# The attention bias of a diffusion trunk: mask laid down by ScalarE, table added by accumulating transfers from GpSimd's queue

## The chip, the core and the metric

One core of one Trainium2 chip. The metric is the device time of one execution of the whole program in microseconds (us), the median of several runs. TensorE (PE) does the matrix products, VectorE (DVE), ScalarE (ACT) and GpSimd (POOL) the elementwise work, SyncE (SP) issues nearly all transfers. Each engine takes its instructions in a fixed order and stops at the first one whose inputs are not there.

## The reference, cut to what matters

Two layers of a trunk over 256 latent tokens (a grid of 4 rows and 64 columns) and 256 context tokens, 1024 wide. A layer is a half-step SwiGLU, a mixer, and another SwiGLU; each is normed and modulated by vectors that come from a product of the conditioning with `ada_w`. One part of the mixer is neighbourhood attention with six heads, and its scores get a bias from a small table, with a mask on columns that are too far:

```python
col_ok = (col[None, :] >= c0[:, None]) & (col[None, :] < c0[:, None] + NA_COLS)
d_row = row_idx - r[:, None]
d_col = jnp.clip(col[None, :] - col[:, None], 1 - NA_COLS, NA_COLS - 1)
bias = rpb[:, d_row[:, None, :, None] + NA_ROWS - 1, d_col[None, :, None, :] + NA_COLS - 1].astype(jnp.float32)
bias = jnp.where(col_ok[None, None, :, None, :], bias, MASK_VALUE).reshape(h, rows, GRID_W, n_keys)
s_lat = jnp.einsum('bhrqd,bhrkd->bhrqk', qg, kg).astype(jnp.float32) * scale + bias
```

All arithmetic is float32. The mask is finite (-1e30), so mask plus table value is the mask again.

## The kernel before, in words

**Weights.** Each product is made of three matmuls of split operands: a weight tile `raw` comes in by SP (line 96, three buffers), ScalarE rounds it to its high part `whi` (line 109), VectorE subtracts to get the low part `wlo` (line 110), and TensorE runs lines 224, 225 and 226. Units are converted a few ahead of their use.

**The start.** SP issues, in this order: the identity (a first slice of the constants `cc`), the tokens, eight tiles `adaraw` of `ada_w`, two `raw` tiles, eight more `adaraw`, then the rest of `cc` (line 1139, 1056 KB, which holds the column mask), the sinks, a third `raw` tile, and the table copied 64 times into DRAM scratch `scr` (line 1035, once for each layer). Meanwhile ScalarE squares the tokens, and the reciprocal norms are spread over the partitions: TensorE makes them a row (line 1264), ScalarE copies that row to `rbc` (line 1266, once for the latents and once for the context). Then for each of four blocks of modulation, TensorE multiplies (`adaps`, line 314), ScalarE evicts (`adaev`, line 317), TensorE turns the result (`adap`, line 320), VectorE adds (`mod`, line 298). With `rbc` and `mod` VectorE makes `xn` (line 1281) and ScalarE `h` (line 1283), and the first products of the first SwiGLU start. The blocks come in two pairs; half of the first products lie between the pairs.

**Later modulation** runs beside the products: VectorE multiplies and sums tiles `adaraw` into `adaacc` (lines 347, 349), in a side stream that `tick` advances by a credit for each unit of products.

**The bias.** `load_bias` stands in that side stream, once for each layer, behind the first jobs. `bias` is one tile of 12 pieces (head and half of the queries) of 128 x 256, used for both layers. 24 transfers from SP (line 1041) place the table, each 64 partitions by 4 rows of 64 elements from `scr`, shifted by one element from partition to partition. Then one addition on GpSimd (line 1044) adds the column mask to all of it. The attention reads it on VectorE (line 893); it runs in the mixer, 537 us after the start in the first layer.

**What sets the order.** A scheduler orders each engine's instructions by the order of the program and by what its own model takes to be ready; it moves the pieces of `load_bias` far ahead of the place where they are written. On GpSimd, the mixer's linear attention has its products with `tot` (line 778) and the zeroing of `atbd` (lines 819, 820), which ScalarE then fills (line 821); later come the preparation of `hp` and `ssq` (lines 1215, 1233, 1234).

Of the kernel before, what the change touches and what calls it, by code (L numbers as in the profile page):

```python
# [10 lines left out]
AF = mybir.ActivationFunctionType  # L11
OP = mybir.AluOpType
# [55 lines left out]
class Stream:  # L68
    """Weights in the order of their use: loaded ahead, split into float32r high and low parts ahead."""

# [43 lines left out]
    def pump(self, n=1):  # L114
        """Split up to n more units, no further ahead than the limit."""
        while n > 0 and self.done_conv < min(self.pos + self.au, len(self.units)):
            with Prio(self.K.tc, self.late):
                self.convert()
            n -= 1
# [9 lines left out]
def merge(*streams):  # L129
    """Interleave generators that yield their cost: each (generator, expected total)."""  # L130
    live = [[g, max(tot, 1e-6), 0.0] for g, tot in streams]
    while live:
        s = min(live, key=lambda e: e[2] / e[1])
        try:
            s[2] += next(s[0])
        except StopIteration:
            live.remove(s)


def weave(*streams):  # L140
    """Like merge, of generators that yield None while they wait for what another one traces."""
    live = [[g, max(tot, 1e-6), 0.0] for g, tot in streams]
    while live:
        for s in sorted(live, key=lambda e: e[2] / e[1]):
            try:
                c = next(s[0])
            except StopIteration:
                live.remove(s)
                break
            if c is not None:  # L150
                s[2] += c
                break
        else:
            raise AssertionError("nothing can go on")
# [12 lines left out]
class Prio:  # L167
    """Instructions traced inside count as d places later (or earlier) in the order of the program."""

# [26 lines left out]
class Kern:  # L196
# [30 lines left out]

# [1 line left out]
    def plan(self):  # L229
# [51 lines left out]

# [1 line left out]
    def ada_load(self, l, blk, q):  # L283
        """Two of the eight row chunks of a block of 512 columns."""
        src = self.ins["ada_w"]
        r = self.slot([128, 2, 512], F32, "adaraw")
        off = src[l].offset + q * 256 * 9216 + blk * 512
        self.nc.sync.dma_start(r, bass.AP(tensor=src.tensor, offset=off,
                                          ap=[[9216, 128], [128 * 9216, 2], [1, 512]]))
        return r  # L290

    def ada_put(self, l, m, bs, src):
        """mod = sums + ada_b for halves bs of m; src is [128, 4, len(bs), 2]."""
        nb = len(bs)
        col = l * 72 + m * 8 + 4 * bs[0]
        b = self.adab[:, col:col + 4 * nb].rearrange("p (b c) -> p c b", b=nb)
        dst = self.mod[l][:, m, 4 * bs[0]:4 * bs[0] + 4 * nb, :].rearrange("p (b c) t -> p c b t", b=nb)
        self.nc.vector.tensor_tensor(out=dst, in0=src, in1=b[:, :, :, None].to_broadcast([128, 4, nb, 2]), op=OP.add)
        ds = slice(4 * bs[0], 4 * bs[0] + 4 * nb)
        if m in (1, 4, 7):  # L300
            c0 = l * 24 + (m // 3) * 8
            g = self.normg[:, c0 + ds.start:c0 + ds.stop]
            self.nc.vector.scalar_tensor_tensor(self.modA[l][:, m // 3, ds, :], self.mod[l][:, m, ds, :], 1.0,
                                                g[:, :, None].to_broadcast([128, 4 * nb, 2]), op0=OP.add, op1=OP.mult)
        if m in (2, 8):
            self.nc.vector.tensor_scalar(self.mod[l][:, m, ds, :], self.mod[l][:, m, ds, :], 0.5, None, op0=OP.mult)

    def ada_direct(self, l, blk, raws):
        """All products on the tensor engine: four column groups take the row chunks in turn."""
        nc = self.nc  # L310
# [12 lines left out]
    def ada_gen(self, l, ms):  # L323
        """Products and sums over the row chunks on the vector engine, sums over partitions on the tensor engine."""
        nc = self.nc
# [63 lines left out]

# [1 line left out]
    def rstd(self, ps, n, scale):  # L391
        """1/sqrt(ps * scale + eps) for n columns of PSUM."""
        nc = self.nc
# [24 lines left out]
    def first(self, norm, us, segs, take, more=None):  # L418
        """Products of the first units after a norm. Those of the latents are of x * g * (1 + scale) and of the shift
        beside it, and the rest of the norm is applied to them; those of the context are of the normed chunks."""  # L420
        if norm.boot is not None:
# [51 lines left out]

# [1 line left out]
    def ffn(self, l, j, norm, nxt):  # L475
# [81 lines left out]
    def tail(self, units, prod, l, m, nxt):  # L557
        """The last chunks of a sublayer, one token segment after the other, with the first's norm under the second."""
        self.preload(AF.Sqrt, self.eps[:, 0:1])
# [12 lines left out]
    def preload(self, func, src):  # L572
        """Have the table of a function loaded ahead of its use, after src is there."""
        t = self.small("preload")
        self.nc.scalar.activation(t[:, 0:1], src, func)

# [1 line left out]
    def proj(self, h, n):  # L578
# [83 lines left out]
    def stack_q(self, src, n, scale):  # L662
        """Per head of a pair: its high part on its own 64 partitions, its low part on the other 64."""
        nc = self.nc
# [8 lines left out]
    def stack_k(self, src, copies):  # L673
        """Per head of a pair: its high part on both halves of the partitions; its low part on its own or both."""
        nc = self.nc
# [186 lines left out]
    def attention(self, l, R, kind):  # L862
        """Software-pipelined over (pair of heads, tile of queries)."""
        nc = self.nc
# [164 lines left out]
    def load_bias(self, l):  # L1029
        """bias[q, k] = rpb[row(k) - row(q) + 7, col(k) - col(q) + 15] + column mask, by copies one element apart."""  # L1030
        nc = self.nc
        src = self.ins["na_rpb"]
        n = 6 * 15 * 31
        scr = self.dram.tile([64, n], F32, tag="scr", name="scr")
        nc.sync.dma_start(scr, bass.AP(tensor=src.tensor, offset=src[l].offset, ap=[[0, 64], [1, n]]))
        for qt in range(2):
            for r in range(2):
                off = scr.offset + (7 - (2 * qt + r)) * 31 + 15
                dst = self.bias[r * 64:r * 64 + 64, qt:12:2, :].rearrange("p h (a b) -> p h a b", a=4)
                for h in range(6):  # L1040
                    nc.sync.dma_start(dst[:, h], bass.AP(tensor=scr.tensor, offset=off + h * 465,
                                                         ap=[[n - 1, 64], [31, 4], [1, 64]]))
                    yield 0.25
        nc.gpsimd.tensor_tensor(out=self.bias[:, 0:12, :], in0=self.bias[:, 0:12, :], op=OP.add,
                                in1=self.colmask[:, None, :].to_broadcast([128, 12, 256]))

# [1 line left out]
    def build(self):  # L1048
# [140 lines left out]
class Norm:  # L1189
    """RMSNorm with modulation: h = x * rstd * g * (1 + scale) + shift, in float32r high and low parts."""  # L1190

# [27 lines left out]
    def pre(self, d):  # L1219
        """x * g * (1 + scale) of a chunk of the latents and, after it, the shift, in high and low parts."""  # L1220
        K = self.K
        nc = K.nc
# [20 lines left out]
    def upto(self, s, n):  # L1243
        """Trace the steps of the norm of a segment up to number n: 1 rstd, 2 its row, 3 modulation."""
        while self.stage[s] < n:
# [11 lines left out]
    def spread(self, s):  # L1257
        """rstd, from a column per tile of tokens to a row on all partitions."""
        K = self.K
# [30 lines left out]
class Final(Norm):  # L1290
    """The last RMSNorm: the chunks are scaled by g and turned token-major as they come."""

# [76 lines left out]
```

## Time and profile before

| what | value |
|---|---|
| runs | 1915.71, 1918.98, 1918.99 us; median 1918.98 us |
| profiled execution, first to last instruction | 1913.9 us |
| TensorE busy | 1868.6 us, 98% of the span |
| VectorE busy | 1258.1 us, 66% |
| ScalarE busy | 722.9 us, 38% |
| GpSimd busy | 140.4 us, 7% |
| mean granted TensorE clock | 0.993 |

For the profiled execution the profile gives the span alone, no time of its own beside it; the three runs lie 1.8 to 5.1 us above that span. The busy shares are means over 1.9 ms; what a change is worth is read where an engine stands still. "Idle before" names in brackets how long an engine stood before an instruction and what ended that.

### The profile page before, as it was taken

Reading aid. Unit: us, or ns where it says so; the run is one execution under the profiler, and the core shown is the slowest. Engines: PE = TensorE matmul, PEld = TensorE weight load, DVE = VectorE, ACT = ScalarE, POOL = GpSimd, SP = SyncE. Lnnn points to the kernel's source line nnn. Section 1 sums busy time; section 2 is a strip of 40 time slices with the busy share of each in tenths; the row PEclk is TensorE's granted clock in tenths of the full one; section 3 lists DMA queues with packets and bytes.
Section 4 is the critical chain, followed back from the end, with each engine's and each line's share of the span. In section 5 each row is a group of like instructions: output and inputs, shape, how many; then the busy total and the mean of one; then the engine's idle time right before and its main releaser. Section 6 shows DMA issues by size and latency. Waiting matters only on the chain.

```text
span 1913.9 us, 27639 instructions
## 1 busy us (share of the span) xinstructions
PE 1868.6 (98%) x11023; PEld 1529.9 (80%) x11023; DVE 1258.1 (66%) x2325; ACT 722.9 (38%) x1202; POOL 140.4 (7%) x207
## 2 busy tenths in 40 slices
PE   7989999999999899999999999999999999999998
PEld 4777777889777578787777897777888977789998
DVE  4796758665865778867567675565334767687554
ACT  3332322245345357323222262222123535566443
POOL 0100000030400102000000020000001140020000
PEclk9999999999999999999999999999999999999999
DMA  9765546432311122645446327565222411146651
GB/s 342 201 217 164 164 146 205 147 110 67 89 29 36 33 70 67 220 155 175 146 149 201 121 80 229 156 203 169 88 94 82 124 54 48 31 139 203 214 172 56
DMA packets 233642, 258.24 MB, mean 135 GB/s; under 512 B 18886, under 2 KB 195370, under 8 KB 233258
## 3 DMA queue, kind: packets, MB, share of 16 engines
q1 hardware_dynamic: 233514, 256.48, 42.1%
q8 instruction: 87, 1.43, 0.3%
q14 instruction: 41, 0.34, 0.1%
HBM read 255.41 MB, written 2.48 MB: 135 GB/s over the span
## 4 chain that ended last, share of the span: by engine, by line
PE 91%; DVE 4%; ACT 2%; DMA 1%; issue 1%; SPq 1%; POOL 1%; DVEq 0%; ACTq 0%; POOLq 0%
PE mm L224 27%; PE mm L225 27%; PE mm L226 26%; PE ot L936 2%; PE pt L917 2%; PE s L882 1%; DMA adaraw<-in_ada_w_dram 1%; PE hgo L836 1%; DVE adaacc L349 1%; PE s L881 1%; PE adaps L359 1%; POOL k L778 1%; PE lv L751 0%; DVE tot L785 0%; ACT whi L109 0%
## 5 line engine op out<-in xcount | busy, mean ns | idle before, releaser
L224 PE MATMUL mm<-h,whi 128*128 128x512 f32 (+1 forms) x1632 | 594.8, 365 | 7.0 <-DVE silu L523 4.8
L225 PE MATMUL mm<-h,wlo 128*128 128x512 f32 (+1 forms) x1632 | 589.6, 362 | 0.0
L226 PE MATMUL mm<-h,whi 128*128 128x512 f32 (+1 forms) x1632 | 589.5, 361 | 0.0
L110 DVE TENSOR_TENSOR wlo<-raw,whi 128x1024 fp32r<-128x1024 f32 (+2 forms) x344 | 400.2, 1183 | 91.7 <-ACT whi L109 76.9
L109 ACT ACTIVATE whi<-raw 128x1024 fp32r<-128x1024 f32 (+2 forms) x344 | 338.7, 1012 | 296.4 <-PE mm L225 130.1
L224 PEld LDWEIGHTS mm<-h,whi 128*128 128x128 f32 x1632 | 307.7, 189 | 69.7 <-issue 15.0
L225 PEld LDWEIGHTS mm<-h,wlo 128*128 128x128 f32 x1632 | 307.9, 189 | 50.9 <-issue 2.5
L226 PEld LDWEIGHTS mm<-h,whi 128*128 128x128 f32 x1632 | 307.6, 189 | 50.5 <-issue 0.7
L349 DVE SCALAR_TENSOR_TENSOR adaacc<-adaraw,s,adaacc 128x512 f32<-128x512 f32 x392 | 281.8, 765 | 37.2 <-DMA adaraw<-in_ada_w_dram 35.9
L224 PE MATMUL mm<-g,whi 128*128 128x512 f32 (+1 forms) x740 | 265.3, 359 | 0.0
L226 PE MATMUL mm<-g,whi 128*128 128x512 f32 (+1 forms) x740 | 264.0, 357 | 0.0
L225 PE MATMUL mm<-g,wlo 128*128 128x512 f32 (+1 forms) x740 | 263.8, 357 | 0.0
L219 ACT ACTIVATE g<-silu 128x512 fp32r<-128x512 f32 (+1 forms) x92 | 51.4, 562 | 320.5 <-DVE silu L523 287.9
L523 DVE TENSOR_TENSOR silu<-mm,silu 128x512 f32<-128x512 f32 (+1 forms) x80 | 50.0, 630 | 167.2 <-PE mm L226 142.4
L224 PEld LDWEIGHTS mm<-g,whi 128*128 128x128 f32 x740 | 139.3, 188 | 24.8 <-ACT whi L109 2.5
L415 DVE SCALAR_TENSOR_TENSOR xT<-mm,mod,xT 128x256 f32<-128x256 f32 x216 | 96.7, 478 | 94.6 <-PE mm L226 94.0
L225 PEld LDWEIGHTS mm<-g,wlo 128*128 128x128 f32 x740 | 139.3, 188 | 21.6
L226 PEld LDWEIGHTS mm<-g,whi 128*128 128x128 f32 x740 | 139.3, 188 | 21.6
L1233 POOL CAST hp<-mod 128x2 fp32r<-128x2 f32 x40 | 22.3, 588 | 1073.1 <-PE mm L225 338.9
L522 ACT ACTIVATE silu<-mm 128x512 f32<-128x512 f32 (+1 forms) x80 | 42.7, 548 | 130.5 <-PE mm L226 130.5
L220 DVE TENSOR_TENSOR g<-silu,g 128x512 fp32r<-128x512 f32 (+1 forms) x92 | 54.9, 604 | 31.9 <-ACT g L219 31.6
L1215 POOL TENSOR_TENSOR ssq<-ssq,sq 128x256 f32<-128x256 f32 x50 | 44.4, 902 | 309.5 <-ACT sq L1212 309.3
(213 smaller groups left out, 2016.1 us busy)
## 6 DMA issues: line engine op xcount, KB each, us to landing
raw<-in_ffn_w_dram SPq DMA_DIRECT2D x120, 1024.0 KB, 5.5
adaraw<-in_ada_w_dram SPq DMA_DIRECT2D x144, 512.0 KB, 5.2
raw<-in_ffn_w_dram SPq DMA_DIRECT2D x16, 768.0 KB, 5.2
raw<-in_w_in_dram SPq DMA_DIRECT2D x12, 1024.0 KB, 5.2
raw<-in_w_in_dram SPq DMA_DIRECT2D x16, 512.0 KB, 5.1
raw<-in_w_out_dram SPq DMA_DIRECT2D x8, 640.0 KB, 3.9
bias<-scr SPq DMA_DIRECT2D x48, 64.0 KB, 2.4
raw<-in_w_in_dram SPq DMA_DIRECT2D x4, 768.0 KB, 4.7
```

What stands on the lines that cost most here:

```text
L109: K.nc.scalar.activation(hi, v, AF.Copy)
L110: K.nc.vector.tensor_tensor(out=lo, in0=v, in1=hi.bitcast(F32), op=OP.subtract)
L219: self.nc.scalar.activation(hi, src, AF.Copy)
L220: self.nc.vector.tensor_tensor(out=lo, in0=src, in1=hi.bitcast(F32), op=OP.subtract)
L224: mmul(ps, whi, ahi, start=start, stop=False)
L225: mmul(ps, wlo, ahi, start=False, stop=False)
L226: mmul(ps, whi, alo, start=False, stop=stop)
L349: nc.vector.scalar_tensor_tensor(acc[:, t], w, sc, acc[:, t], op0=OP.mult, op1=OP.add)
L415: self.nc.vector.scalar_tensor_tensor(self.x[:, d, sl], ps[:, sl], self.mod[l][:, m, d, s:s + 1], self.x[:, d, sl], op0=OP.mult, op1=OP.add)
L522: nc.scalar.activation(a[:, 0:n], ps[i][:, 0:n], AF.Silu)
L523: nc.vector.tensor_tensor(out=a[:, 0:n], in0=ps[2 + i][:, 0:n], in1=a[:, 0:n], op=OP.mult)
L1215: eng.tensor_tensor(out=self.ssq[s], in0=self.ssq[s], in1=t, op=OP.add)
```

## The change

`load_bias` no longer adds on GpSimd. Four ScalarE activations first copy the column mask into the bias, three pieces of 256 columns each; the 24 placing transfers move from SP's queue to GpSimd's and add what they bring to what is there. The four new steps also take 2.0 of credit in the side stream. (The change takes comments and docstrings out as well; behind `load_bias`, line numbers are 2 higher.)

```diff
     def load_bias(self, l):
...
         nc.sync.dma_start(scr, bass.AP(tensor=src.tensor, offset=src[l].offset, ap=[[0, 64], [1, n]]))
+        for b in range(0, 12, 3):
+            nc.scalar.activation(self.bias[:, b:b + 3, :], self.colmask[:, None, :].to_broadcast([128, 3, 256]), AF.Copy)
+            yield 0.5
         for qt in range(2):
             for r in range(2):
                 off = scr.offset + (7 - (2 * qt + r)) * 31 + 15
                 dst = self.bias[r * 64:r * 64 + 64, qt:12:2, :].rearrange("p h (a b) -> p h a b", a=4)
                 for h in range(6):
-                    nc.sync.dma_start(dst[:, h], bass.AP(tensor=scr.tensor, offset=off + h * 465,
-                                                         ap=[[n - 1, 64], [31, 4], [1, 64]]))
+                    nc.gpsimd.dma_start(dst[:, h], bass.AP(tensor=scr.tensor, offset=off + h * 465,
+                                                           ap=[[n - 1, 64], [31, 4], [1, 64]]), accum_op=OP.add)
                     yield 0.25
-        nc.gpsimd.tensor_tensor(out=self.bias[:, 0:12, :], in0=self.bias[:, 0:12, :], op=OP.add,
-                                in1=self.colmask[:, None, :].to_broadcast([128, 12, 256]))
```

ScalarE's order at the start, before (`rs` is the reciprocal norm, `preload` loads a function table, `rbc`, `adaev` and `h` as above):

```order
L396 ACTIVATE rs<-ss,eps 128x4
L575 ACTIVATE preload<-eps 128x1
L1266 ACTIVATE rbc<-rbc 128x256 x2
L317 ACTIVATE adaev<-adaps 128x512 x2
L1283 ACTIVATE h<-xn,mod_141 128x256 x4
L109 ACTIVATE whi<-raw 128x1024 x4
```

and with the change, the same stretch:

```order
L396 ACTIVATE rs<-ss,eps 128x4
L575 ACTIVATE preload<-eps 128x1
L1038 ACTIVATE bias<-cc 128x768 x2
L1268 ACTIVATE rbc<-rbc 128x256
L1038 ACTIVATE bias<-cc 128x768
L1268 ACTIVATE rbc<-rbc 128x256
L1038 ACTIVATE bias<-cc 128x768
L317 ACTIVATE adaev<-adaps 128x512 x2
L1285 ACTIVATE h<-xn,mod_141 128x256 x4
L109 ACTIVATE whi<-raw 128x1024 x4
```

Two pieces of the mask stand ahead of the first `rbc`, two more ahead of the first `adaev`. SP's order from the second eight `adaraw` on, before:

```order
L288 DMA adaraw<-in_ada_w_dram 128x2x512 x8
L1139 DMA cc<-in_consts_dram 128x2112
L1142 DMA sink<-in_sw_sink_dram 128x12
L96 DMA raw<-in_ffn_w_dram 128x8x256
L1035 DMA scr<-in_na_rpb_dram 64x2790 x2
L1041 DMA bias<-scr 64x4x64 x5
L96 DMA raw<-in_ffn_w_dram 128x8x256 x2
L1041 DMA bias<-scr 64x4x64 x17
L96 DMA raw<-in_ffn_w_dram 128x8x256
L288 DMA adaraw<-in_ada_w_dram 128x2x512 x2
```

and with the change:

```order
L288 DMA adaraw<-in_ada_w_dram 128x2x512 x8
L1141 DMA cc<-in_consts_dram 128x2112
L1144 DMA sink<-in_sw_sink_dram 128x12
L96 DMA raw<-in_ffn_w_dram 128x8x256
L1036 DMA scr<-in_na_rpb_dram 64x2790 x2
L96 DMA raw<-in_ffn_w_dram 128x8x256 x3
L288 DMA adaraw<-in_ada_w_dram 128x2x512 x2
```

The mask's transfer keeps its place; the placing transfers are gone from this queue. GpSimd's order in the first layer's mixer, before (`k` and `tot` belong to the linear attention):

```order
L778 TENSOR_TENSOR k_3145<-k_3145,tot 128x8x32 x2
L819 MEMSET atbd 64x8x64
L820 MEMSET atbd 64x8x64
L819 MEMSET atbd 64x8x64
L820 MEMSET atbd 64x8x64
L1044 TENSOR_TENSOR bias<-bias,cc 128x3072
L1233 CAST hp<-mod_141 128x2 x2
```

and with the change:

```order
L778 TENSOR_TENSOR k_3146<-k_3146,tot 128x8x32 x2
L1045 DMA bias<-scr 64x4x64 x6
L819 MEMSET atbd 64x8x64
L820 MEMSET atbd 64x8x64
L819 MEMSET atbd 64x8x64
L820 MEMSET atbd 64x8x64
L1045 DMA bias<-scr 64x4x64 x18
L1235 CAST hp<-mod_141 128x2 x2
```

Six of the second layer's transfers now stand ahead of the zeroing of `atbd`; the second layer's four mask pieces lie on ScalarE among this mixer's softmax, the first behind its second exponential.

## Rows read from the trace of the kernel before

**Rows 1.** The page: span and busy time of TensorE.
```profile
span 1913.9 us, 27639 instructions
...
PE 1868.6 (98%) x11023; PEld 1529.9 (80%) x11023; DVE 1258.1 (66%) x2325; ACT 722.9 (38%) x1202; POOL 140.4 (7%) x207
```
**Rows 2.** Waits of TensorE, 60 to 300 us: waited for, total us, times, longest.
```profile
PE mm L224 <- DVE silu L523: 4.8, 1, 4.8
```
**Rows 3.** Waits of TensorE, 600 to 700 us.
```profile
PE pt L917 <- DVE sm L908: 5.0, 1, 5.0
```
**Rows 4.** Timeline of ScalarE, 0 to 60 us: start, length, what, idle before.
```profile
17.44 0.38 ACT L1266 ACTIVATE rbc<-rbc 128x256 f32<-128x256 f32 x1 [4.71 <-PE rbc L1264]
...
21.42 0.60 ACT L317 ACTIVATE adaev<-adaps 128x512 f32<-128x512 f32 x1 [3.02 <-PE adaps L314]
...
26.98 1.71 ACT L1283 ACTIVATE h<-xn,mod 128x256 fp32r<-128x256 f32 x4 [1.34 <-DVE mod L298]
```
**Rows 5.** Timeline of SP's queue, 0 to 100 us.
```profile
28.21 0.53 SPq L1139 DMA_DIRECT2D cc<-in_consts_dram  x1
...
50.94 14.92 SPq L1041 DMA_DIRECT2D bias<-scr  x17
```
**Rows 6.** Line 1139, the transfer that holds the mask: issue to landing.
```profile
DMA to landing us min/median/max: 13.4/13.4/13.4
```
**Rows 7.** ScalarE's groups by shape: the nearest copy of 768 columns.
```profile
L109 ACT ACTIVATE whi<-raw 128x768 fp32r<-128x768 f32 x40 | 31.9, 834 | 13.3 <-PE mm L225 13.3
```
**Rows 8.** Timeline of TensorE, 0 to 60 us.
```profile
17.91 3.43 PE L314 MATMUL adaps<-adaraw,s 128*32 128x512 f32 x16
...
25.69 1.05 PE L320 MATMUL adap<-cc,adaev 128*128 128x2 f32 x8 [0.72 <-ACT adaev L317]
28.33 3.77 PE L314 MATMUL adaps<-adaraw,s 128*32 128x512 f32 x12 [1.59 <-DMA adaraw<-in_ada_w_dram]
...
33.24 0.73 PE L224 MATMUL mm<-h,whi 128*128 128x512 f32 x2
...
38.93 0.95 PE L320 MATMUL adap<-cc,adaev 128*128 128x2 f32 x8
```
**Rows 9.** Timeline of VectorE, 0 to 60 us: the first low parts.
```profile
30.03 4.63 DVE L110 TENSOR_TENSOR wlo<-raw,whi 128x1024 fp32r<-128x1024 f32 x4
```
**Rows 10.** Stretches: us, busy (x) of PE, PEld, DVE, ACT, POOL, granted clock, DMA.
```profile
52.00:62.00 10.00, 10.00 (x37) 8.06 (x38) 8.64 (x15) 5.77 (x9) 0.00 (x0) 0.84 1.01 261
...
104.00:108.00 4.00, 4.00 (x14) 3.11 (x14) 4.00 (x7) 4.00 (x5) 0.00 (x0) 0.71 0.76 273
650.00:656.00 6.00, 5.53 (x23) 3.59 (x24) 3.48 (x13) 1.29 (x5) 0.18 (x1) 0.51 0.00 0
```
**Rows 11.** All that touches the bias: count, ns min/median/max, first and last start.
```profile
L1041 SPq DMA_DIRECT2D bias<-scr x48: 573/614/1756, 46.3 to 640.4; - x48
L893 DVE CUSTOM_DVE_ANT_1 sb<-s,bias x22: 672/692/693, 536.9 to 1639.5; 128x512 f32<-128x512 f32 x22
...
L1044 POOL TENSOR_TENSOR bias<-bias,cc x2: 6933/7154/7374, 81.8 to 643.2; 128x3072 f32<-128x3072 f32 x2
```
**Rows 12.** Timeline of VectorE, 58 to 125 us.
```profile
73.27 0.88 DVE L347 TENSOR_SCALAR adaacc<-adaraw,s 128x512 f32<-128x512 f32 x2 [7.32 <-DMA adaraw<-in_ada_w_dram]
74.07 4.06 DVE L349 SCALAR_TENSOR_TENSOR adaacc<-adaraw,s,adaacc 128x512 f32<-128x512 f32 x6
...
81.05 9.95 DVE L349 SCALAR_TENSOR_TENSOR adaacc<-adaraw,s,adaacc 128x512 f32<-128x512 f32 x5
```
**Rows 13.** Timeline of VectorE, 630 to 660 us.
```profile
643.68 6.65 DVE L909 TENSOR_SCALAR P<-P,sm 128x256 f32<-128x256 f32 x1
```
**Rows 14.** Timeline of GpSimd, 530 to 760 us.
```profile
554.46 0.52 POOL L819 MEMSET atbd<- 64x512 f32 x1 [46.47 <-PE kTps L795]
```
**Rows 15.** Timeline of ScalarE, 536 to 580 us.
```profile
541.34 0.71 ACT L904 ACTIVATE P<-sb,sm 128x512 f32<-128x512 f32 x1
...
557.28 0.63 ACT L821 ACTIVATE atbd<-at 64x512 f32<-64x512 f32 x1
```

## The prediction

> **What bounds the kernel now.** The page comes first: TensorE is busy for 98% of the span [rows 1]. So a stretch in which TensorE stands still is lost for good, and work on another engine costs nothing until TensorE waits for it. TensorE's own waits therefore come second. After the start only two are of any length: 4.8 us for VectorE's `silu` [rows 2] and 5.0 us for a `sm` of the softmax [rows 3]. Both are traces of GpSimd's additions to the bias: these last 6.9 and 7.4 us, from 81.8 us and from 643.2 us on [rows 11], and beside them five `adaacc` steps take 9.95 us, where six took 4.06 us shortly before [rows 12], and one small scaling takes 6.65 us [rows 13]. VectorE is held by the addition, and TensorE then waits for VectorE. The third look is at the start (ScalarE's and TensorE's timelines): there a chain rules that goes norm row, `rbc`, `adaps`, `adaev`, `mod`, `h`, first products, and every link stands on the order of one engine.
>
> **Part 1: the mask pieces on ScalarE at the start.** In ScalarE's order the first two pieces stand ahead of the first `rbc`. They read the part of `cc` that SP requests at 28.21 us [rows 5] and that takes 13.4 us to land [rows 6]: the mask is there at 41.6 us. Nothing ahead of that transfer in SP's order changes, so I keep this moment. In the kernel before, `rbc` ran at 17.44 us [rows 4]; ScalarE will now stand still in front of it. A piece is 768 columns; the nearest row, a copy of 768 columns, takes 0.83 us [rows 7], and I take 0.8. So `rbc` comes at 41.6 + 2 x 0.8 = 43.2 us, 25.8 us late.
>
> What follows? The first `adaps` starts at 17.91 us, just behind the first `rbc` (17.44 + 0.38), and ends at 21.34, when `adaev` starts [rows 4, 8]; I take it that `adaps` waits for `rbc`. The other two pieces (1.6 us) then lie beside `adaps` and cost nothing. Up to `h` all is 25.8 us late: 26.98 + 25.8 = 52.8 us [rows 4]. From there some of it comes back. Before, TensorE waited 1.59 us for `adaraw` and spent 28.33 to 33.24 us on `adaps` between arrivals, so the first product began 6.3 us after `h` [rows 4, 8]; with the change these tiles have long landed. Now the low parts of the weights limit: four of them, done by VectorE at 30.03 + 4.63 = 34.7 us [rows 9], and now at 60.5 us. Between 33.24 us and the next `adap` at 38.93 us lie 24 matmuls, 0.237 us each [rows 8]; in TensorE's order, which is the same in both kernels here, seven of them stand behind the fourth low part. So that `adap` comes at 60.5 + 7 x 0.237 = 62.2 us, 23.3 us late. Behind it nothing gives any back: both kernels have the same order and all transfers of the start have landed.
>
> TensorE also comes out of a long idle time. After a shorter one, before 52 us, the granted clock over the next 10 us was 0.84 [rows 10], so part of it ran at 1.2 instead of 2.4 GHz, worth 10 x 0.16 = 1.6 us. I add that. **Loss at the start: 23.3 + 1.6 = 24.9 us.** Lower end 21.8 us (23.3 less 1.5, if `adaps` doesn't wait for `rbc`); upper end 25.8 + 1.6 = 27.4 us (nothing comes back).
>
> **Part 2: GpSimd's additions go.** First layer: VectorE gets back what it lost at 81 us, 9.95 us less five steps of 4.06 / 6 us, that is 6.6 us [rows 12], more than the 4.8 us that TensorE waited. SP's queue helps: before, 17 placing transfers held it from 50.94 us for 14.92 us [rows 5], and VectorE waited 7.32 us for the `adaraw` behind them [rows 12]. So I count the whole wait, 4.8 us, and the slow clock behind it, 4 us at 0.71, 1.2 us [rows 2, 10]: 6.0 us. Second addition: 5.0 us of waiting [rows 3] and 5.5 busy us at a clock of 0.51, 2.7 us [rows 10]: 7.7 us. **Gain: 6.0 + 7.7 = 13.7 us**, with a lower end of 0, if something else is late at the same places.
>
> **Part 3: the four mask pieces in the mixer.** 4 x 0.8 us on ScalarE, which is idle more than it works there; each waits for readers of the bias that the next exponential needs too. I count one piece, 0.8 us, in the softmax chain, 0 to 3.2 us as bounds.
>
> **Part 4: 48 accumulating transfers from GpSimd.** The trace has none. The nearest row is the same transfer issued by SP: 0.61 us, at most 1.76 us [rows 11]. In the first layer 24 of them start when scratch and mask are there, and the attention reads the bias at 536.9 us [rows 11]: even at ten times SP's time they are hidden. In the mixer six go ahead of the zeroing of `atbd`. The first piece lies behind the second exponential, at about 541.3 + 0.8 = 542.1 us; the zeroing ran at 554.46 us, and ScalarE's filling, which waits for it, at 557.28 us [rows 14, 15]. So there is room for (557.3 - 0.5 - 542.1) / 6 = 2.4 us each. I take SP's longest, 1.76 us, and cost this at nothing; beyond 2.4 us it becomes a rival below. The other 18 have only `hp` behind them, much later. The 2.0 of credit move a few `adaacc` steps by a place: nothing, give or take 1 us.
>
> The Trainium skill (SBUF — State Buffer, section Who interferes with whom) says that GpSimd's writing of transfer descriptors needs a port pair that VectorE takes whole in its two-port modes, so that such a transfer looks stalled. No run here shows it for transfers. By that rule the six would take longer than by SP's row, and the sum would be the second rival's.
>
> **Sum.** 24.9 - 13.7 + 0.8 = +12.0 us. The profiled span of 1913.9 us [rows 1] becomes 1925.9 us. The runs lie 1.8 to 5.1 us above that span; I add the sum to their median: 1918.98 + 12.0 = **1931.0 us**. Ends: 1918.98 + 21.8 - 13.7 = 1927.1 us and 1918.98 + 27.4 + 3.2 = 1949.6 us.
>
> **The rivals.** *Faster: ScalarE isn't held at the start.* Then only parts 2 and 3 stand, 1918.98 - 12.9 = 1906.1 us. It decides at 15.8 us: a mask landed by then would let both pieces end before `rbc` at 17.44 us. For it: in the kernel before nothing waits for this transfer at the start. Against it: the order of ScalarE and of SP, and a landing 26 us after that point. 7%.
>
> *Slower still: GpSimd's queue in the mixer.* If one transfer takes 4.0 us instead of 2.4, ScalarE stands 6 x 1.6 = 9.6 us in front of `atbd`, with softmax and weight conversion behind it; TensorE has a few us of products left, so 6 us show, and the clock behind such a wait costs 2 us more, as at 650 us [rows 10]. 1931.0 + 8 = 1939 us. For it: VectorE is busy there and has held or been held by GpSimd in this trace [rows 13]. 12%.
>
> *The gains don't come*, because VectorE stays the last at these places, or the new transfers hold it as the addition did: 1931.0 + 13.7 = 1944.7 us, or half of it, 1938. For it: the `adaacc` steps fill VectorE around 80 to 110 us anyway. 9%.
>
> *It evens out*: the loss is at its lower end and more than 13.7 us comes back, since SP and the weights run ahead while TensorE stands. TensorE's idle time after the start is hardly more than the two waits that I have counted, so there is little left to regain. About 1920 us, 5%.
>
> **How the numbers follow.** My forecast has the remaining 67%. A measurement of this kernel can tell about 0.2%, 3.8 us, from no change. Faster by more: 7%. Within: 5%. Slower by more: 88%. The range for 8 in 10 holds the forecast with its lower end, somewhat less for a little more regained, and the second and third rival's centres: 1923 to 1944 us.
>
> **What would show it.** At the start, ScalarE stands still from 12.7 us to about 41.6 us, waiting for `cc`; the first `rbc` is at 43 us, `h` at 53 us, the first products near 56 us, and TensorE's idle time before 60 us grows by over 20 us. At 80 to 110 us TensorE waits no more for `silu`, and in the mixer no scaling takes 6 us. GpSimd is busy 14 us less with additions. Were `rbc` still at 17 us, part 1 would be wrong and the kernel faster; were ScalarE to wait for GpSimd at `atbd`, part 4.

## The result and the profile after

| | before | with the change |
|---|---|---|
| median | 1918.99 us (4 runs, 1915.71 to 1919.32) | 1926.92 us (4 runs, 1926.44 to 1928.35) |
| profiled execution, span | 1913.9 us | 1924.7 us |
| its mean granted clock | 0.993 | 0.989 |

The ratio is 1.0053 with an interval of 1.0041 to 1.0066: the change makes the kernel slower by half a per cent, as predicted; 1931.0 us was forecast, with a range of 1923 to 1944 us. The kernel before spreads more than its first three runs show: in the two later comparisons its medians were 1916.55 us (9 runs) and 1916.26 us (13 runs, 1913.22 to 1918.69).

The page of the kernel with the change, span and busy times (before: [rows 1]):

```profile
span 1924.7 us, 27674 instructions
...
PE 1867.5 (97%) x11023; PEld 1528.8 (79%) x11023; DVE 1245.7 (65%) x2325; ACT 729.5 (38%) x1210; POOL 178.2 (9%) x253
```

TensorE works as long as before, to within 1.1 us, in a span that is 10.8 us longer: the time is in its standing still. Where it comes from, and where some of it goes back, is read from one operation that recurs in the same order in both kernels, VectorE's update of the tokens `xT`. The rows of this line, before, over the whole span and from two places on (count, ns min/median/max, first and last start in us):

```profile
L415 DVE SCALAR_TENSOR_TENSOR xT<-mm,mod,xT x216: 457/477/486, 145.6 to 1904.5; 128x256 f32<-128x256 f32 x108
...
L415 DVE SCALAR_TENSOR_TENSOR xT<-mm,mod,xT x12: 467/478/486, 663.9 to 691.6; 128x256 f32<-128x256 f32 x12
L415 DVE SCALAR_TENSOR_TENSOR xT<-mm,mod,xT x12: 473/476/484, 978.2 to 1008.8; 128x256 f32<-128x256 f32 x12
```

and the same three with the change:

```profile
L415 DVE SCALAR_TENSOR_TENSOR xT<-mm,mod,xT x216: 457/479/489, 162.8 to 1915.2; 128x256 f32<-128x256 f32 x108
...
L415 DVE SCALAR_TENSOR_TENSOR xT<-mm,mod,xT x8: 465/482/483, 672.1 to 689.1; 128x256 f32<-128x256 f32 x8
L415 DVE SCALAR_TENSOR_TENSOR xT<-mm,mod,xT x8: 474/478/484, 987.7 to 1004.9; 128x256 f32<-128x256 f32 x8
```

The first starts, and the last one of the first row, belong to the same update in both. So the change is 17.2 us late at 146 us, 8.2 us late behind the first mixer (664 us), 9.5 us late at 978 us, and 10.7 us late at the last update. Before 146 us there is one more point: the second pair's `adap`, at 38.93 us before [rows 8] and now at 62.61 us, 23.7 us late. The account by these points, with what the prediction had:

| stretch | predicted | measured |
|---|---|---|
| start, up to the second pair's `adap` | +24.9 | +23.7 |
| from there to 146 us (first addition gone) | -6.0 | -6.5 |
| to 664 us (second addition gone, mask pieces in the mixer) | -7.7 + 0.8 | -9.0 |
| 664 to 978 us | 0, give or take 1 | +1.3 |
| 978 us to the last update | 0 | +1.2 |
| sum | +12.0 | +10.7 |

**The start.** ScalarE's timeline with the change (start, length, what, idle before); [rows 4] hold the same steps of before:

```profile
40.25 1.58 ACT L1038 ACTIVATE bias<-cc 128x768 f32<-128x768 f32 x2 [27.41 <-DMA cc<-in_consts_dram]
41.73 0.36 ACT L1268 ACTIVATE rbc<-rbc 128x256 f32<-128x256 f32 x1
...
43.00 0.84 ACT L1038 ACTIVATE bias<-cc 128x768 f32<-128x768 f32 x1
43.73 0.59 ACT L317 ACTIVATE adaev<-adaps 128x512 f32<-128x512 f32 x1
...
51.54 1.71 ACT L1285 ACTIVATE h<-xn,mod 128x256 fp32r<-128x256 f32 x4 [1.34 <-DVE mod L298]
```

Line 1141, the transfer with the mask (before: 13.4 us, [rows 6]):

```profile
DMA to landing us min/median/max: 11.9/11.9/11.9
```

And TensorE's timeline beside it ([rows 8] before):

```profile
17.89 3.21 PE L314 MATMUL adaps<-adaraw,s 128*32 128x512 f32 x16
44.38 1.86 PE L320 MATMUL adap<-cc,adaev 128*128 128x2 f32 x8 [23.28 <-ACT adaev L317]
46.17 3.35 PE L314 MATMUL adaps<-adaraw,s 128*32 128x512 f32 x16
...
54.25 0.50 PE L224 MATMUL mm<-h,whi 128*128 128x512 f32 x1 [1.09 <-ACT whi L109]
...
55.86 0.76 PE L225 MATMUL mm<-h,wlo 128*128 128x512 f32 x1 [0.17 <-DVE wlo L110]
...
62.61 0.95 PE L320 MATMUL adap<-cc,adaev 128*128 128x2 f32 x8
```

ScalarE stands 27.41 us in front of the first two pieces, until `cc` has landed. Both `rbc` copies and the first `adaev`, which need nothing of the mask, stand behind them. The first `adaps` did not wait: it ran at 17.89 us, as before. What waited was its eviction, and TensorE behind it for 23.28 us in one piece.

**The two waits that went.** TensorE's longest wait from 60 to 300, from 600 to 700 and from 860 to 990 us (waited for, total us, times, longest):

```profile
PE mm L224 <- ACT h L1285: 1.6, 1, 1.6
...
PE ot L936 <- ACT ptsb L920: 0.8, 1, 0.8
...
PE adap L366 <- ACT adaev L362: 0.8, 1, 0.8
```

The 4.8 us for `silu` [rows 2] and the 5.0 us for `sm` [rows 3] are gone, and nothing has taken their place. VectorE's five `adaacc` steps that took 9.95 us [rows 12] take 3.40 us (VectorE's timeline; its first line, the low parts of the start, is spoken of further down):

```profile
54.59 4.62 DVE L110 TENSOR_TENSOR wlo<-raw,whi 128x1024 fp32r<-128x1024 f32 x4
...
90.44 4.06 DVE L349 SCALAR_TENSOR_TENSOR adaacc<-adaraw,s,adaacc 128x512 f32<-128x512 f32 x6
...
98.57 3.40 DVE L349 SCALAR_TENSOR_TENSOR adaacc<-adaraw,s,adaacc 128x512 f32<-128x512 f32 x5
```

**A third place.** Of the 9.0 us gained between 146 and 664 us, 7.5 lie behind 638 us, where the second addition stood (ScalarE's `qs`, at 637.7 us before, is 15.7 us late). The other 1.5 us come near 500 us, in the linear attention, where TensorE waits for `q` (line 778). Its waits of this kind from 300 to 520 us, before and with the change:

```profile
PE lv L751 <- DVE q L778: 2.4, 2, 1.4
PE lv L751 <- DVE q L778: 0.9, 1, 0.9
```

The prediction has nothing there. ScalarE's instructions beside this wait stand in another order with the change. Of the versions below, the one with the pieces made late has the short wait too (0.8 us), the ones with the early mask and without additions have the long one (2.4 us); which edit moves the order stays open.

**GpSimd's queue.** Its timeline, with the first layer's 24 transfers, the first six of the second layer and the zeroing of `atbd` behind them ([rows 14] before):

```profile
45.69 24.95 POOL L1045 DMA_DIRECT2D bias<-scr  x24 [44.81 <-DMA scr<-in_na_rpb_dram]
...
557.77 6.36 POOL L1045 DMA_DIRECT2D bias<-scr  x6 [32.59 <-ACT bias L1038]
570.14 0.52 POOL L819 MEMSET atbd<- 64x512 f32 x1 [6.00 <-PE kTps L795]
```

Six transfers took 6.36 us, 1.06 us each; then GpSimd stood idle for 6.00 us, waiting for TensorE's `kTps`. The zeroing was not held.

### The profile page after: what moved, and what is told of

The parts are those of the page before. It is cut to its first block, busy times and chain, and to the rows that moved or that the text cites. A ratio compares the mean times of both kernels' runs of the same rounds, so it can differ in the third digit from the quotient of the medians.

```text
span 1924.7 us, 27674 instructions
## 1 busy us (share of the span) xinstructions
PE 1867.5 (97%) x11023; PEld 1528.8 (79%) x11023; DVE 1245.7 (65%) x2325; ACT 729.5 (38%) x1210; POOL 178.2 (9%) x253
## 3 DMA queue, kind: packets, MB, share of 16 engines
q1 hardware_dynamic: 220458, 253.33, 40.8%
## 4 chain that ended last, share of the span: by engine, by line
PE 93%; ACT 2%; DMA 2%; DVE 1%; issue 1%; POOL 1%; SPq 0%; DVEq 0%; ACTq 0%; POOLq 0%
PE mm L224 28%; PE mm L225 27%; PE mm L226 27%; PE ot L936 2%; PE pt L917 1%; PE s L882 1%; PE hgo L836 1%; DMA adaraw<-in_ada_w_dram 1%; PE s L881 1%; PE adaps L359 1%; PE lv L751 1%; DMA cc<-in_consts_dram 1%; POOL k L778 1%; PE adap L366 0%; ACT whi L109 0%
## 5 line engine op out<-in xcount | busy, mean ns | idle before, releaser
L349 DVE SCALAR_TENSOR_TENSOR adaacc<-adaraw,s,adaacc 128x512 f32<-128x512 f32 x392 | 275.0, 749 | 33.7 <-DMA adaraw<-in_ada_w_dram 32.4
```

What stands on the lines that cost most here:

```text
L349: nc.vector.scalar_tensor_tensor(acc[:, t], w, sc, acc[:, t], op0=OP.mult, op1=OP.add)
```

## The experiments

The theory: the pieces' place on ScalarE, ahead of `rbc` and behind a late transfer, costs some 24 us; the end of GpSimd's additions gives 13 to 14 us back; the two have nothing to do with each other. The rivals: the gain comes from the transfers leaving SP's queue; or it comes from the standstill itself, in which VectorE and the queues run ahead, so that a change without the standstill would gain less. The "drift" below is the lateness against the profiled execution of before at the updates of `xT`, as above; ratios are those to runs of before on the same chip.

### The pieces, but not ahead of the start

First by making the first layer's four pieces read a zero that VectorE derives from the last `h` of the start (the lines that keep `h` and make `late` are left out):

```diff
...
+        if l == 0:
+            nc.vector.tensor_scalar(self.late, self.h0[KC - 1][:, 1, TOK - 1:TOK].bitcast(F32), 0.0, None, op0=OP.mult)
...
-            nc.scalar.activation(self.bias[:, b:b + 3, :], self.colmask[:, None, :].to_broadcast([128, 3, 256]), AF.Copy)
+            src3 = self.colmask[:, None, :].to_broadcast([128, 3, 256])
+            if l == 0:
+                nc.scalar.activation(self.bias[:, b:b + 3, :], src3, AF.Identity, bias=self.late)
+            else:
+                nc.scalar.activation(self.bias[:, b:b + 3, :], src3, AF.Copy)
```

> The change, but in the first layer the four mask pieces on ScalarE also read a zero that VectorE makes from the last h of the start, so that they come after the start's chain; the accumulating transfers stay on GpSimd's queue. Theory (ScalarE stands before the first rbc until the mask lands, and that is the whole loss of 23.7 us): the first rbc is back near 17.5 us, the loss is gone and the two gains stay, 6.5 us at 80 to 110 us and 8.8 us in the first mixer: about 1919 - 14 = 1905 us. Rival (the loss comes from the transfers on GpSimd's queue, which lie in the same stretch): 1920 to 1927 us, and the first products stay late.

Measured: 1904.03 us (5 runs), ratio 0.9935 (0.9922 to 0.9947), span 1902.3 us. Its ScalarE timeline has `rbc` back where it was before:

```profile
17.36 0.38 ACT L1275 ACTIVATE rbc<-rbc 128x256 f32<-128x256 f32 x1 [4.71 <-PE rbc L1273]
```

Second by leaving the pieces first in the order and making the mask early, in a transfer of its own, fourth in SP's order:

```diff
         nc.sync.dma_start(cc[:, C_B2:C_END], I["consts"][:, C_B2:C_END])
+        nc.sync.dma_start(cc[:, C_COL:C_SW], I["consts"][:, C_COL:C_SW])
...
-        nc.sync.dma_start(cc[:, 128:C_B2], I["consts"][:, 128:C_B2])
+        nc.sync.dma_start(cc[:, C_SW:C_B2], I["consts"][:, C_SW:C_B2])
```

> The change, but the 256 columns of the mask come in a transfer of their own, fourth on SP's queue, ahead of the tokens; the rest of the constants stays where it was. Theory: the pieces find the mask there and run before the squares of the tokens, 3 us of ScalarE that the norm chain partly feels (rbc 0 to 2 us late); the wait of 27 us is gone and both gains stay: 1904 to 1908 us. Rival (transfers on GpSimd's queue make the loss): 1920 to 1927 us.

Measured: 1904.57 us (5 runs), ratio 0.9939 (0.9926 to 0.9951), span 1900.9 us. The pieces (count, ns, first and last start), and ScalarE's timeline:

```profile
L1038 ACT ACTIVATE bias<-cc x8: 825/828/849, 5.6 to 634.2; 128x768 f32<-128x768 f32 x8
```

```profile
18.20 0.38 ACT L1269 ACTIVATE rbc<-rbc 128x256 f32<-128x256 f32 x1 [3.74 <-PE rbc L1267]
```

The first piece runs at 5.6 us, ahead of the first squares of the tokens, and `rbc` is 0.8 us late instead of 24. Two different ways of removing the standstill give the same time, 22 to 23 us below the change (ratios of 0.9935 and 0.9939 against 1.0053): the standstill is the whole loss. And without it the gain stays: the drift is -6.7 and -6.5 us at 146 us, -15.5 and -14.0 us at 664 us (the 1.5 us between the two are those near 500 us). The rival of the standstill falls. Both versions beat both kernels.

### The additions alone, the queue alone, the pieces alone

Before without GpSimd's addition. The column mask is then missing in the bias:

```diff
-        nc.gpsimd.tensor_tensor(out=self.bias[:, 0:12, :], in0=self.bias[:, 0:12, :], op=OP.add,
-                                in1=self.colmask[:, None, :].to_broadcast([128, 12, 256]))
```

> The kernel before without the addition on GpSimd; the column mask is left out of the bias, all else is as it was, the transfers on SP's queue too. Theory (the additions hold VectorE and are the source of both gains): VectorE's steps of 10 and 6.7 us are gone, TensorE no longer waits 4.8 us for silu nor 5.0 us in the mixer, 1904 to 1907 us. Rival (the gain is SP's queue, freed of 48 transfers): the mixer's gain may come, but the first layer's does not, TensorE still waits for silu near 100 us: 1909 to 1913 us.

Measured: 1902.24 us (4 runs), ratio 0.9927 (0.9914 to 0.9941), span 1900.1 us. The drift is -6.5 us at 146 us, -13.8 us at 664 us, and -13.8 us at every later point: 6.5 + 7.3 us is what two additions cost, and it is all that the change has to gain, but for the 1.5 us near 500 us. (1904 to 1907 us was expected, from the first runs of before; from the 1916.55 us beside this run, 13.8 us less are 1902.8 us.) VectorE's timeline in this kernel:

```profile
72.94 0.89 DVE L347 TENSOR_SCALAR adaacc<-adaraw,s 128x512 f32<-128x512 f32 x2 [6.92 <-DMA adaraw<-in_ada_w_dram]
...
80.72 3.40 DVE L349 SCALAR_TENSOR_TENSOR adaacc<-adaraw,s,adaacc 128x512 f32<-128x512 f32 x5
```

SP still carries the placing transfers here, and VectorE still waits 6.92 us for the `adaraw` behind them (7.32 before, [rows 12]). It does no harm as long as nothing holds VectorE afterwards.

Before with its placing transfers on GpSimd's queue, not accumulating, and the addition kept:

```diff
-                    nc.sync.dma_start(dst[:, h], bass.AP(tensor=scr.tensor, offset=off + h * 465,
+                    nc.gpsimd.dma_start(dst[:, h], bass.AP(tensor=scr.tensor, offset=off + h * 465,
```

> The kernel before with its 48 placing transfers on GpSimd's queue instead of SP's, plain ones, and GpSimd's addition as before; ScalarE gets no mask pieces. Theory (in the first layer either is enough: the addition gone, or SP free so that VectorE's adaraw tiles come 7 us earlier; in the mixer only the addition counts): TensorE no longer waits for silu near 100 us, 6.5 us, but still waits 5 us in the mixer: about 1910 us against 1916.6 us of the kernel before. Rival (the addition alone counts in both places): 1915 to 1918 us, and the wait near 100 us stays. Second rival (transfers on GpSimd's queue cost time in themselves): above 1919 us.

Measured: 1911.21 us (8 runs), ratio 0.9976 (0.9966 to 0.9986), span 1909.1 us. TensorE's longest wait from 600 to 700 us, VectorE's timeline near 75 us, and the transfers (count, ns, first and last start):

```profile
PE pt L917 <- DVE P L909: 3.7, 1, 3.7
```

```profile
69.50 0.88 DVE L347 TENSOR_SCALAR adaacc<-adaraw,s 128x512 f32<-128x512 f32 x2 [2.91 <-DMA adaraw<-in_ada_w_dram]
...
76.69 6.14 DVE L349 SCALAR_TENSOR_TENSOR adaacc<-adaraw,s,adaacc 128x512 f32<-128x512 f32 x1 [1.12 <-DMA adaraw<-in_ada_w_dram]
```

```profile
L1041 POOL DMA_DIRECT2D bias<-scr x48: 615/615/802, 48.0 to 635.7; - x48
```

The addition still holds VectorE (one `adaacc` step takes 6.14 us), but with the placing transfers gone from SP's queue the `adaraw` steps start at 69.50 instead of 73.27 us [rows 12], and TensorE's wait for `silu` shrinks from 4.8 to 0.5 us. From the second pair's `adap`, 0.5 us late, to 146 us, 3.7 us early, this version gains 4.2 us, where the one without additions gains 6.5. In the mixer nothing of the kind helps: of the wait of 5.0 us, 3.7 stay. So in the first layer the wait had two causes in a row, a late `adaraw` and a held VectorE, and either of them taken away removes most of it; in the mixer it had one.

Before with the first layer's four pieces put in, and all else kept (the copied mask is overwritten by the placing transfers):

```diff
+        if l == 0:
+            for b in range(0, 12, 3):
+                nc.scalar.activation(self.bias[:, b:b + 3, :], self.colmask[:, None, :].to_broadcast([128, 3, 256]), AF.Copy)
+                yield 0.5
```

> The kernel before, with nothing but the four mask pieces of the first layer added on ScalarE; they stand ahead of rbc and adaev as in the change, and the transfers on SP write over them, and GpSimd's addition stays. Theory: the loss alone, 23.7 us less what an earlier run of SP gives back (none): 1940 to 1944 us, rbc near 42 us. Rival (GpSimd's transfers make the loss): 1918 to 1921 us.

Measured: 1935.05 us (4 runs), ratio 1.0092 (1.0077 to 1.0107), span 1933.6 us. TensorE's longest waits before 60 us and from 600 to 700 us, and then ScalarE's, VectorE's and GpSimd's timelines:

```profile
PE adap L320 <- ACT adaev L317: 23.7, 2, 23.0
...
PE pt L917 <- DVE sm L908: 4.9, 1, 4.9
```

```profile
40.30 1.58 ACT L1038 ACTIVATE bias<-cc 128x768 f32<-128x768 f32 x2 [27.29 <-DMA cc<-in_consts_dram]
...
90.79 0.88 DVE L347 TENSOR_SCALAR adaacc<-adaraw,s 128x512 f32<-128x512 f32 x2
...
96.68 7.98 DVE L220 TENSOR_TENSOR g<-silu,g 128x512 fp32r<-128x512 f32 x2 [1.04 <-ACT g L219]
...
97.26 6.85 POOL L1048 TENSOR_TENSOR bias<-bias,cc 128x3072 f32<-128x3072 f32 x1 [96.39 <-ACT g L219]
```

The start loses 23.6 us (the second pair's `adap`, at 62.54 us), with no accumulating transfer in the kernel, and the mixer keeps its wait, both as they should; the rival, that GpSimd's transfers make the loss, falls. But the kernel came out 5 to 9 us below the 1940 to 1944 us that were expected, and the drift says where: it is 18.8 us at 146 us already, so 4.8 us have come back. (Some 2.5 us of the miss are the base: the runs of before beside this one have a median of 1916.55 us.) The addition still holds VectorE, whose `g` takes 7.98 us instead of 1.3 for two, and TensorE does not wait for `silu`. SP's 17 placing transfers are through at 74.4 us, VectorE comes to its `adaacc` steps at 90.79 us, late itself, and finds `adaraw` there (before it waited 7.32 us for it [rows 12]); it is the same "either removes most of it" as above. So behind the late start some 5 us come back by themselves, because the first layer's addition has become harmless. The loss and the first layer's gain are not two independent terms: the standstill costs 18.8 us at 146 us where the addition is kept, and 17.2 + 6.5 = 23.7 us where it is gone (the change against the versions without a standstill). Behind the standstill, the end of the first addition is worth 1.6 us (18.8 - 17.2), no more than single profiles differ by.

### Smaller questions

Is the loss halved if the mask lands half as late? The whole rest of `cc` is requested ahead of the second eight `adaraw`:

```diff
         self.st._dma(1)
+        nc.sync.dma_start(cc[:, 128:C_B2], I["consts"][:, 128:C_B2])
         raws.update({(blk, q): self.ada_load(0, blk, q) for blk in (3, 1) for q in range(4)})
...
-        nc.sync.dma_start(cc[:, 128:C_B2], I["consts"][:, 128:C_B2])
```

> The change with the whole second part of the constants, mask included, requested ahead of SP's second eight adaraw tiles instead of behind them, so that it lands about 13 us earlier, near 27 us. The scheduler answers by putting all four mask pieces ahead of the squares of the tokens on ScalarE. Theory (what counts is which of ScalarE's instructions stand behind the pieces): the squares, 5 us, and the norm chain now come behind the landing too, rbc near 38 us instead of 41.7 us, and the loss falls only by 3 to 5 us: 1921 to 1924 us. Rival (only the landing counts): rbc near 29 us, the loss falls by 12 us: 1913 to 1916 us.

Measured: 1928.37 us (4 runs), ratio 1.0057 (1.0043 to 1.0070), span 1926.9 us: no better than the change. ScalarE's timeline, and TensorE's longest wait before 60 us:

```profile
29.69 3.04 ACT L1038 ACTIVATE bias<-cc 128x768 f32<-128x768 f32 x4 [23.90 <-DMA cc<-in_consts_dram]
...
40.82 0.38 ACT L1268 ACTIVATE rbc<-rbc 128x256 f32<-128x256 f32 x1 [2.23 <-PE rbc L1266]
```

```profile
PE rbc L1266 <- DVE rs L402: 24.5, 1, 24.5
```

The mask lands 10.6 us earlier, and `rbc` comes 0.9 us earlier. Neither expectation came: the mask landed at 29.7 us and not near 27, and `rbc` came at 40.8 us and not near 38. That the squares stand behind the pieces was foreseen: with the transfer elsewhere the scheduler put all four pieces ahead of the squares of the tokens too, so the norms themselves stood behind the mask. What counts is not the wait alone, but which instructions stand behind it.

Is the 1.3 us between 664 and 978 us the credit of the four new steps? The early mask again, with the steps taking none:

```diff
             nc.scalar.activation(self.bias[:, b:b + 3, :], self.colmask[:, None, :].to_broadcast([128, 3, 256]), AF.Copy)
-            yield 0.5
```

> The version with the mask in an early transfer of its own, and the four mask pieces no longer take credit in the side stream. Theory (the credit moves the products of the second layer's modulation, which costs 1.1 us near 940 us): that wait of TensorE is gone, 1 us less than the early mask with the credit, 1903 to 1904 us, and the profiled span 1900 us. Rival (the 1.1 us come from the transfers on GpSimd): no difference to the early mask with the credit, 1904.5 us, and the wait near 940 us stays.

Measured: 1903.34 us (5 runs), ratio 0.9932 (0.9918 to 0.9945), span 1902.9 us. The wait for `adap` of 0.8 us between 860 and 978 us, which the change has, is gone, and the drift stays where it is between 860 and 978 us (-12.6 and -12.5 us). All five kernels that spend the credit rise there by 1.0 to 1.1 us (the change, both versions with an early `rbc`, the pieces alone, the mask in the middle); the three that don't (this one, no addition, queue alone) rise by at most 0.1. In the total this is not to be seen: the interval overlaps that of the kernel with the credit. The span of 1900 us that was expected did not come either: this execution is the slowest of the five, its granted clock from 50 to 60 us is 0.66, where the early mask has 1.00, and it is only 4.3 us early at 146 us.

## Why the prediction was right, and where it was not

**The mechanism** was the predicted one, link by link: ScalarE stood from 12.8 us until the mask had landed, `rbc` came at 41.7 us (43.2 forecast), `h` at 51.5 us (52.8), and the waits for `silu` and `sm` went.

**Part 1, the mask's landing.** The moment was taken over from before, 41.6 us; it was 40.25 us, since the transfer took 11.9 us instead of 13.4. A piece took 0.84 us (0.8 taken), and pieces in a row follow each other every 0.74 us.

**Part 1, "I take it that `adaps` waits for `rbc`".** This step failed. `adaps` ran at its old time; the row that I had read it from, a start just behind the first `rbc` [rows 4, 8], showed only that the two were neighbours in time. So the first `adaev` was not 25.8 but 43.73 - 21.42 = 22.3 us late, behind all four pieces and both `rbc`. The lower end of the range had this case, priced at 1.5 us; it made 3.5.

**Part 1, what comes back, and the clock.** This was the second miss, and it went the other way. TensorE came out of its standstill at half its clock, and it was ahead of `h` that this counted first: the first `adap` took 1.86 us and the second `adaps` 3.35 us (TensorE's timeline above). The same two in TensorE's timeline of the kernel before:

```profile
22.07 1.05 PE L320 MATMUL adap<-cc,adaev 128*128 128x2 f32 x8 [0.73 <-ACT adaev L317]
23.05 1.92 PE L314 MATMUL adaps<-adaraw,s 128*32 128x512 f32 x16
```

That is 0.8 + 1.4 = 2.2 us; so `h` was 22.3 + 2.2 = 24.5 us late (51.54 - 26.98). Stretches of the kernel with the change (us, busy (count) of PE, PEld, DVE, ACT and POOL, granted clock, DMA):

```profile
40.00:50.00 10.00, 5.14 (x24) 2.37 (x24) 1.22 (x4) 4.47 (x8) 4.31 (x7) 0.55 0.80 244
...
54.00:59.00 5.00, 4.14 (x10) 2.84 (x11) 5.00 (x6) 4.32 (x7) 5.00 (x11) 0.69 0.80 76
...
658.00:664.00 6.00, 6.00 (x46) 3.92 (x44) 4.09 (x15) 2.62 (x10) 5.86 (x6) 1.00 0.63 52
```

From 40 to 50 us the granted clock was 0.55 and from 54 to 59 us 0.69, so much of both ran at 1.2 instead of 2.4 GHz. Behind `h`, 3.5 us came back at first: the first product began 2.7 us after `h` (54.25 - 51.54) instead of 6.3. Of that 1.0 us went again while TensorE stood in front of the first high and low parts, so 2.5 us came back, as counted. But the low parts did not set the pace behind that, as the working has it: TensorE waited 0.17 us for the first one and for no other. From there to the next `adap` it had no gap, and took 62.61 - 55.86 = 6.75 us where it had taken 38.93 - 33.81 = 5.12: the slow clock, 1.6 us more. In sum 22.3 - 2.5 + 2.2 + 1.6 = 23.6 us, with the rounding the 23.7 us measured; the forecast had 25.8 - 2.5 + 1.6 = 24.9 us. Two errors worked against each other, 3.5 us too much for the wait and 2.2 us too little for the clock; that the sum of this part came so close is in part luck.

**Part 2.** 6.0 and 7.7 us were counted. With nothing else in the way the additions cost 6.5 and 7.3 us (the kernel without them), 13.8 us against 13.7: the wait plus the slow clock behind it, both from rows, was the right price of the additions. In the mixer the clock was 0.51 before [rows 10] and is 1.00 now at the same place. What the prediction did not see ("Behind it nothing gives any back", it says of the start) is that in the first layer the late start alone does nearly the same (the pieces alone: 4.8 us back up to 146 us, with the addition kept; the change: 6.5). So in the change most of these 6 us would have come back with the addition in place. That did no harm to the sum, because either cause gives most of the same gain, but the term came out right by luck.

**Part 3.** One piece in the softmax was counted, 0.8 us. The early mask, with pieces and accumulating transfers in the mixer, gains 7.5 us between 146 and 664 us, and the kernel without either 7.3 us (both with the long wait near 500 us): the four pieces cost nothing there that shows.

**Part 4.** Nothing was counted for the 48 transfers, with 1.76 us each as the value taken and 2.4 us as the point where it turns. They took 1.04 to 1.06 us. The second rival (1939 us, 12%) falls by that and by the 6.00 us that GpSimd had to spare. 24 of them went out in 24.95 us from 45.69 us on, while VectorE did the four low parts in 4.62 us (4.63 before, [rows 9]); six went out in 6.36 us beside the softmax. What gives way there is VectorE, and little: its scalings of 128x512 in the mixer (count, busy us, mean ns, idle before), before, from 300 to 640 us, ahead of the addition:

```profile
L909 DVE TENSOR_SCALAR P<-P,sm 128x512 f32<-128x512 f32 x10 | 4.8, 484 | 0.1
```

and with the change, from 540 to 670 us, beside 24 transfers:

```profile
L909 DVE TENSOR_SCALAR P<-P,sm 128x512 f32<-128x512 f32 x12 | 6.2, 526 | 0.1
```

The mean is 42 ns higher, 0.5 us for all twelve, and it lies in two of them: one took 0.83 us (641.19 us) and one 0.63 us (658.98 us), each among six transfers (from 640.55 and from 657.52 us on), the other ten at most 0.51 us. Beside the addition a single scaling took 6.65 us [rows 13]. The Trainium skill (SBUF — State Buffer, Who interferes with whom) has the writing of descriptors blocked by VectorE's two-port modes; no stall of the queue shows in these rows, so its rule made no difference to the time here.

**The credit.** "Nothing, give or take 1 us": it was 1.1 us, one wait for a later `adap`.

**The end.** The last 1.2 us come at about 1578 us, where the clock was 0.83 for 10 us and TensorE was busy for 7.96 us of them; at the same work before, 10 us earlier, it was busy for 7.99 us at a clock of 1.00. Three other versions have this fall, and four versions and the kernel before do not (last section); that one of the edits releases it is not shown.

**The base.** The sum of +12.0 us against +10.7 us is 1.3 us of the miss of 4.1. Most of the rest is in the last line of the sum: it was added to the median of three runs, 1918.98 us, while the durations came from one execution with a span of 1913.9 us. In the later runs the time lies 1.7 to 1.9 us above the span, so this execution was the run of 1915.71 us. Added to that, the forecast would have been 1927.7 us.

The other rivals: ScalarE was held, so 1906.1 us did not come, though that is within 3 us of what the change gives once it is not held (1904.0 and 1904.6 us). The gains came. And it did not even out, though what this rival builds on, that SP runs ahead while TensorE stands, did act in the first layer (the pieces alone).

## What to carry to other kernels

Putting work on an engine that is idle most of the time is not free where its order is fixed: read what the new instruction waits for and which instructions stand behind it, and either load its input first or tie it to something late; here that turned a loss of 0.5% into a gain of 0.6%. Price a removed wait together with the slow clock behind it, and ask for each wait whether it has two causes in a row: then the first cure takes most of the gain and the second gets little. Add a sum from a profiled execution to that execution's own time, and read a dependency from the order and the code, never from two starts that lie close together.

## What the runs showed of the hardware that was not expected

- An accumulating transfer from GpSimd's queue costs more than a plain one of the same shape on the same queue: one every 1.04 us (24 in 24.95 us) against 0.615 us, and a median of 4.8 us from issue to landing against 2.4 us. The row of the transfers with the change:

```profile
L1045 POOL DMA_DIRECT2D bias<-scr x48: 1006/2512/6293, 45.7 to 660.6; - x48
...
DMA to landing us min/median/max: 2.9/4.8/12.8
```

  The durations in this row overlap: their median is 2.5 us, while 24 together took 24.95 us.

- Falls of the granted clock cost some 1.5 us of drift each and come and go between profiles, at two places of the work. One is near 725 us with the pieces made late (0.87 over 10 us), near 735 us with the queue alone (0.83 over 10 us) and near 755 us with the mask in the middle (0.83 over 10 us). The other is near 1578 us with the change (0.83 over 10 us), near 1556 us in the version without credit (0.86 over 12 us) and with the pieces made late (0.83 over 10 us), and near 1583 us with the mask in the middle (0.83 over 10 us). Taken back by the drift, these are about 742 and 1569 us of the kernel before, which has 1.00 there, as have the kernel without additions and the early mask. At both places TensorE has short gaps, with or without the fall (8.5 and 8.0 of 10 us busy before). What it did before them was not found to differ, and their cause stays open. Differences under 2 us between single profiles are not read here for that reason, the credit's excepted, which eight profiles show alike, and those near 500 us, where the wait itself is in the rows.
